# Eight of a mixer's sixteen sample states: from the second FFN's folded down products into the mixer, by ScalarE and accumulating DMAs

## The chip, the core and the metric

The kernel runs on one core of a Trainium2 chip. The metric is the device time in microseconds. The core's engines, as the profile names them: PE (TensorE, matrix products; PEld is its weight load), DVE (VectorE), ACT (ScalarE), POOL (GpSimd) and SP (SyncE, which issues most DMAs). Each engine works through its own instructions in their order and waits for others by semaphores.

## What is computed

One step of a hybrid decoder block in fp32, on 512 new tokens of a prompt and 8 sample tokens (520 columns in all), D = 1024:

```python
h = h + 0.5 * swiglu(rms_norm(h, ffn1_norm), w1_gate, w1_up, w1_down)      # FFN width 2816
m, new_pool, new_conv, new_ssm = mixer(rms_norm(h, mix_norm), states...)   # pooling heads and SSD heads
h = h + m
h = h + 0.5 * swiglu(rms_norm(h, ffn2_norm), w2_gate, w2_up, w2_down)
return rms_norm(h, final_norm), new_pool, new_conv, new_ssm
```

For each of the 8 sample tokens the SSD mixer has a state of 16 heads x 64 x 128 numbers, which one step renews: `new = exp(dt * A) * state + (dt * x) (outer product) B`. The new state is an output of its own: nothing in the step reads it, since the sample's `y` is computed from the old state and a dot product. The kernel keeps the state of sample `b` as 8 blocks of [128 partitions, 128]; blocks 0 to 3 are group g = 0 and blocks 4 to 7 are g = 1. A "state" below is one pair (b, g): 4 blocks, 256 KB. There are sixteen.

## The kernel before

Columns are handled in two halves of 260. Every fp32 product is made of three fp32r products: a weight is split into a rounded high part (ScalarE cast) and a low part (the difference), and `mm3` (L145 to L150) issues high x high, high x low and low x high. Weights come as raw 512 KB tiles, loaded by SP into a small ring of buffers (`raw_pair`, L101).

The order of the program is: FFN 1, mixer, FFN 2, final norm. A scheduler places the instructions on each engine; some are pinned by `keep_in_program_order`, and the plan strings fix the order in which the stages are written down.

**The FFNs** (`Ffn`, `stream` L534). A gate/up tile `f` (0 to 21) is computed with a two-by-two block scheme of seven products: sums of the raw weight blocks (L412 to L415), split like the weights (`shi`, `slo`), and one separate quarter of the weights (`qs`, `quarter` L432). The low part of that quarter is made either by VectorE (L237) or, for the tiles listed in `LOW_BY_DMA` (L39), by ScalarE writing the negated high part and an accumulating DMA on POOL's queue that adds the raw weights (`part_by_dma`, L230 to L233). Low parts of a tile's first weights are made by accumulating DMAs, too (L382). After tile 7 and after tile 15 the down products of the eight gate tiles before are done in the same scheme: four "folded down" tiles `Down(c, d)`, c = 0 or 1, d = 0 to 3. The last down products (`down_by_half`, L612) are plain.

**The mixer.** Its weights go through `inproj` (L879): cast, low part, 48 matmuls. `conv` (L965) makes x tiles 0 to 7 and B, C: VectorE multiplies and adds (L977), ScalarE's silu writes `X` (L979, L980). `ssd_a` (L1152) prepares one chunk and group (c, g): PE transposes B and X (`px`, L1163, 4 transposes), SP loads `ab` (L1165, three buffers), POOL subtracts (`we`, L1169), ScalarE makes the exponentials (`E` L1175, L1180, L1185, L1186), VectorE multiplies (L1193), POOL makes `xw` (L1191). `ssd_b` (L1196) has the products (`yo`, `pst`, `yd`), and POOL and VectorE update the running state `hst` (L1214, L1215). Chunks of g = 1 read x tiles 4 to 7. `sample(b, g)` (L1088) makes the sample's `y`: SP loads C's row (`cb`) and the old state (`h0`), VectorE multiplies (L1094), ScalarE sums along the row (L1097, with its output thrown away into `junk`). All this is written in the order of two strings, `CONV_PLAN` (L41) and `GATE_PLAN` (L44): `z` is a gate projection, `p`, `c`, `m` pooling, `A` and `B` the SSD parts, `s` samples, `G` and `H` the gate, `o` and `g` output projections.

**The sixteen new states** (`new_states`, L1109) are made in FFN 2. A call of the generator takes one state further: POOL's queue loads B's row, spread over partitions (`br`, L1119), and the old state (`room`, L1120); ScalarE makes `x * dt * B` for the four blocks (`so`, L1139); VectorE does `state * decay + so` (L1141); POOL's queue stores it (`out_nss`, L1143). `STATES` (L38) says where calls stand: one ahead of each of the folded down tiles (both c), one at each of the tiles 6, 17, 19, 20 and 21, and four in the last down products. The first call only loads.

Of the kernel before, what the change touches and what calls it, by code (L numbers as in the profile page):

```python
# [10 lines left out]
F32 = mybir.dt.float32  # L11
F32R = mybir.dt.float32r
AF = mybir.ActivationFunctionType
ALU = mybir.AluOpType
# [3 lines left out]
P = 128  # L18
D = 1024
SEQ = 512  # L20
NS = 8
NT = SEQ + NS
# [12 lines left out]
CHUNKS = (8, 8, 6)  # L35
LOW_ON_DVE = ((2, 0), (3, 0), (KF - 1, 1))
ON_ACT = 4
STATES = ((1, 1, 1, 1), (6, 17, 19, 20, 21), 4)  # L38
LOW_BY_DMA = {1: (2, 3, 4, 5, 6), 2: (*range(7), 9, 11)}  # L39

CONV_PLAN = (  # L41
    "b0 b1 d0 b2 b3 x0 x1 v0 d1 x2 x3 d2 X0 p0 y0 c0 A0 k0 p1 x4 m0 x5 B0 c1 p2 m1 A1 x6 c2 A2 B1 x7 X1 m2 A3"
)
GATE_PLAN = (  # L44
    "z0 B2 A4 z1 B3 p3 z2 B4 s2 z3 c3 A5 s2 z4 m3 B5 s2 A6 z5 e0 s2 G0 z6 A7 z7 B6 s2 o0 H0 s2 o1 B7 s2 o2 s2 G1 "
    "o3 g0 g1 H1 g2 g3"
)
LAST_PLAN = "h0 h2 h1 n0 h3 n1 n2 n3"
SAMPLE_U = 3 + SEQ
# [14 lines left out]
def tile_trunk_step(ctx: ExitStack, tc: tile.TileContext, ins: dict, outs: dict):  # L64
    nc = tc.nc
# [5 lines left out]
    act = ctx.enter_context(tc.tile_pool(name="act", bufs=1, side="left"))  # L71
# [184 lines left out]
    class Ffn:  # L256
# [277 lines left out]
        def stream(self, before, last_chunk):  # L534
            tiles = []
            for f in range(self.direct, KF):
                tiles.append(f)
                if f and f <= self.folded and f % CHUNKS[0] == 0:
                    tiles.extend(Down(f // CHUNKS[0] - 1, d) for d in range(KD // 2))
            prev = None  # L540
            for t in tiles:
                for _ in range(STATES[0][t.d] if not isinstance(t, int) else t in STATES[1]):
                    next(self.states, None)
                self.product(t, 1)
                if prev is not None:
                    self.product(prev, 4)
                for k, p in enumerate((2, 5, 6, 3, 7) if t in (2, KF - 1) else (5, 6, 3, 7, 2)):
                    if k == 1 and prev is not None:
                        self.close(prev)
                    self.product(t, p)  # L550
                self.gates(t)
                if t == 5 and self.later:
                    with queued(*ends[1:]):
                        self.later.pop()()
                prev = t
            self.product(KF - 1, 4)
            with tc.high_priority():
                self.close(KF - 1)
            wd = before()
            if wd is None:  # L560
                self.down(len(CHUNKS) - 1, self.folded, KF, last_chunk)
            else:
                self.down_by_half(len(CHUNKS) - 1, self.folded, last_chunk, wd)
# [48 lines left out]
        def down_by_half(self, c, lo, after, wd):  # L612
            n = KF - lo
            banks, units = {}, []
            for d in range(KD):
                if d < STATES[2]:
                    next(self.states)
# [46 lines left out]
    wx1, g1 = pool("wx1", "right"), pool("g1", "right")  # L664
# [116 lines left out]
    g2 = f2["ffn"].gp = pool("g2", "left")  # L781
# [16 lines left out]
    todo, late = [], []  # L798
# [49 lines left out]
def mixer(tc, ins, outs, e):  # L848
    nc = tc.nc
    cst, act, wp, tmp, dr, pool = (e[x] for x in ("cst", "act", "wp", "tmp", "dr", "pool"))  # L850
# [4 lines left out]
    xh, xl, _, r = nx2[0]  # L855
    xa = e["xa"][0]
    mp = pool("mx", "right")
# [191 lines left out]
    sdec = cst.tile([P, NX, NS], F32, tag="sdec", name="sdec")  # L1049
    sxdt = cst.tile([P, NX, NS], F32, tag="sxdt", name="sxdt")  # L1050
    ysm = mp.tile([P, NX, NS], F32, tag="ysm", name="ysm")
    sbc = mp.tile([P, 2, NS], F32, tag="sbc", name="sbc")
    junk = act.tile([P, NT], F32, tag="acc", name="junk")[:, :P]
    scr_bc = dr.tile([NS, 512], F32, name="scr_bc")

    def rows_bc(b, a, g):
        return scr_bc.rearrange("b (a g n) -> b a g n", a=2, g=2)[b, a, g].unsqueeze(0).to_broadcast([P, P])
# [30 lines left out]
    def sample(b, g):  # L1088
        cb = tmp.tile([P, HB], F32, tag="ta", name=f"cb{b}{g}")[:, :P]
        nc.sync.dma_start(out=cb, in_=rows_bc(b, 1, g))  # L1090
        h0 = mp.tile([P, 4, P], F32, tag="h0", bufs=4, name=f"h0_{b}{g}")
        nc.sync.dma_start(out=h0, in_=ins["state_ssm"][:, b, 4 * g : 4 * g + 4])
        tc.keep_in_program_order(
            nc.vector.tensor_tensor(out=h0, in0=h0, in1=cb.unsqueeze(1).to_broadcast([P, 4, P]), op=ALU.mult))  # L1094
        for q in range(4):
            tc.keep_in_program_order(
                nc.scalar.activation(out=junk, in_=h0[:, q], func=AF.Copy,  # L1097
                                     accum_out=ysm[:, 4 * g + q, b : b + 1]))

    def sample_y(g):  # L1100
# [8 lines left out]
    def new_states(room):  # L1109
# [10 lines left out]
            tc.keep_in_program_order(nc.gpsimd.dma_start(out=hs, in_=ins["state_ssm"][:, b, 4 * g : 4 * g + 4]))  # L1120
            return br, hs

        todo = [(b, g) for g in range(2) for b in range(NS)]
        ahead = []
        for i, (b, g) in enumerate(todo):
            if not ahead:
# [4 lines left out]
            br, hs = ahead.pop(0)  # L1131
            if "hg" in f2:
                o = f2["hg"].tile([P, 4, P], F32, tag="so", bufs=2, name=f"so{b}{g}")
            else:
                o = bank(f"so{b}{g}").rearrange("p (q n) -> p q n", q=4)
            for q in range(4):
                j = 4 * g + q
# [5 lines left out]
            tc.keep_in_program_order(nc.gpsimd.dma_start(out=outs["nss"][:, b, 4 * g : 4 * g + 4], in_=hs))  # L1143
        yield

    e["f2"]["states"] = new_states


# [137 lines left out]
    def outs_a():  # L1286
        nc.sync.dma_start(out=outs["ncp"], in_=ncp)
        nc.sync.dma_start(out=outs["ncs"], in_=sconv)
        nc.sync.dma_start(out=outs["npp"], in_=npp)
        nc.sync.dma_start(out=outs["nps"], in_=spool)  # L1290
# [20 lines left out]
        "h": lambda j: wout(cats[1], 2, j, fin),  # L1311
        "n": fill,
        "e": lambda j: outs_a(),
    }

    def run(plan):
# [98 lines left out]
```

## Time and profile before

| | |
|---|---|
| median of 3 runs | 964.78 us (963.81 to 965.73) |
| the profiled execution | 965.28 us |
| its span, first to last instruction | 963.5 us |
| granted TensorE clock, mean | 0.997 |
| busy PE / DVE / ACT / POOL | 949.7 / 850.3 / 640.7 / 142.9 us |

The span runs through FFN 1 (to about 340 us), the mixer with its output projections (about 340 to 610) and FFN 2 (to the end). The folded down tiles of FFN 1 with c = 0 lie within 80 to 160 us, those of FFN 2 with c = 0 within 680 to 760, and those with c = 1 within 820 to 880. In the view by windows each row holds the stretch, its length, then busy us and number of instructions of PE, PEld, DVE, ACT and POOL, the granted clock, the mean busy share of the DMA engines and GB/s. A timeline row holds start, duration, engine, line, operation, `out<-in`, shapes and, in brackets, idle time of the engine ahead of it and what ended that. A chain row holds start, duration, and what the time went to. A row of the DMA list ends with the size of one DMA and the median us from issue to landing.

### The profile page before, as it was taken

What the parts mean: (1) busy time and instruction counts of PE and PEld (TensorE: products, weight loads), DVE (VectorE), ACT (ScalarE), POOL (GpSimd) and SP (SyncE); (2) the same over time, 40 slices, a digit from 0 to 9 for tenths busy, and PEclk for the clock granted to TensorE, in tenths of its full rate; (3) what the DMA queues carried; (4) which work ended last, traced back from release to release, by engine and by line L of the source; (5) the groups of instructions that cost most, each with busy time, mean ns of one, the idle gap of its engine ahead of it and who ended that gap; (6) DMA issues with size and microseconds to landing.
All of it is one profiled execution on the core that took longest, in us unless ns stands there. A gap on an engine that the chain in (4) does not pass through costs nothing.

```text
span 963.5 us, 19707 instructions
## 1 busy us (share of the span) xinstructions
PE 949.7 (99%) x7676; PEld 930.3 (97%) x7676; DVE 850.3 (88%) x1456; ACT 640.7 (66%) x1208; POOL 142.9 (15%) x228
## 2 busy tenths in 40 slices
PE   9999999999999999999999999999999999999995
PEld 8999999999999999999999999999999999999995
DVE  6899899998997788789978897999889999999886
ACT  7777656676566455485676565677676676766763
POOL 0111101001010001055241000112112101122120
PEclk9999999999999999999999999999999999999998
DMA  7665654545534243362353333447656655666642
GB/s 210 182 167 145 152 156 111 138 136 143 163 112 129 73 142 110 94 199 92 117 159 121 115 117 114 117 121 166 170 154 178 154 146 147 166 192 174 187 141 90
DMA packets 53631, 137.30 MB, mean 142 GB/s; under 512 B 7641, under 2 KB 15769, under 8 KB 53537
## 3 DMA queue, kind: packets, MB, share of 16 engines
q1 hardware_dynamic: 39840, 104.18, 33.4%
q0 software_dynamic: 13424, 31.73, 17.2%
q8 instruction: 60, 0.98, 0.4%
q14 instruction: 35, 0.28, 0.1%
q10 hardware_dynamic: 272, 0.13, 0.0%
HBM read 128.67 MB, written 7.34 MB: 141 GB/s over the span
## 4 chain that ended last, share of the span: by engine, by line
PE 29%; DVE 11%; issue 4%; ACT 3%; DMA 3%; POOL 0%; DVEq 0%; ACTq 0%; POOLq 0%
PE A L150 3%; PE A L146 3%; PE A L149 3%; PE BE L149 3%; PE BE L146 2%; PE BE L150 2%; DMA raw<-in_w2d 2%; PE wo L146 2%; PE wo L150 2%; PE wo L149 2%; PE dh L150 1%; PE dh L146 1%; PE dh L149 1%; ACT junk L1097 1%; PE P L295 1%
## 5 line engine op out<-in xcount | busy, mean ns | idle before, releaser
L476 ACT COPY ac<-A 128x260 f32<-128x260 f32 x85 | 31.7, 373 | 34.8 <-PE A L150 33.6
L412 DVE TENSOR_TENSOR s<-raw 128x1024 f32<-128x1024 f32 x39 | 47.5, 1219 | 2.9 <-DMA raw<-in_w1gu 1.3
L476 ACT COPY ac<-BE 128x260 f32<-128x260 f32 x41 | 15.4, 376 | 30.0 <-PE BE L150 29.0
L146 PE MATMUL inx<-xh_mx,whi_inx 128*128 128x260 f32 x112 | 31.8, 284 | 0.0
L149 PE MATMUL inx<-xl_mx,whi_inx 128*128 128x260 f32 x112 | 31.6, 282 | 0.0
L150 PE MATMUL inx<-xh_mx,wlo_inx 128*128 128x260 f32 x112 | 31.6, 282 | 0.0
L977 DVE SCALAR_TENSOR_TENSOR A<-U,h,A 128x544 f32<-128x544 f32 x36 | 28.9, 802 | 1.3 <-ACT A L975 0.9
L295 PE MATMUL P<-x,raw 128*128 128x260 f32 x128 | 28.6, 384 | 0.0
L295 PEld LDWEIGHTS P<-x,raw 128*128 128x128 f32 x128 | 24.2, 191 | 4.0 <-DMA raw<-in_w1gu 0.4
L146 PE MATMUL wo<-catg,whi_wo 128*128 128x260 f32 x96 | 27.7, 289 | 0.0
L150 PE MATMUL wo<-catg,wlo_wo 128*128 128x260 f32 x96 | 27.2, 284 | 0.0
L149 PE MATMUL wo<-catg,whi_wo 128*128 128x260 f32 x96 | 27.1, 282 | 0.0
L1097 ACT ACTIVATE junk<-h 128x128 f32<-128x128 f32 x64 | 19.8, 309 | 10.5 <-DVE h L1094 9.0
L1139 ACT ACTIVATE so<-br,sxdt 128x128 f32<-128x128 f32 x64 | 22.5, 375 | 4.6 <-DVE room L1141 4.6
L150 PE MATMUL A<-xth_f,qs 128*128 128x260 f32 x84 | 23.8, 283 | 0.7 <-DMA qs<-in_w2gu 0.7
L146 PE MATMUL A<-xth_f,qs 128*128 128x260 f32 x84 | 23.8, 284 | 0.0
L1240 DVE TENSOR_TENSOR h<-wo,h 128x260 f32<-128x260 f32 x48 | 19.0, 416 | 5.4 <-PE wo L150 5.4
L149 PE MATMUL A<-xtl_f,qs 128*128 128x260 f32 x84 | 23.7, 282 | 0.0
L237 DVE TENSOR_TENSOR gs<-gq,gs 128x780 fp32r<-128x780 f32 (+1 forms) x28 | 23.2, 827 | 0.4 <-ACT gs L236 0.4
L146 PE MATMUL inz<-xh_mx,whi_inz 128*128 128x260 f32 x80 | 22.9, 287 | 0.0
L149 PE MATMUL inz<-xl_mx,whi_inz 128*128 128x260 f32 x80 | 22.7, 283 | 0.0
L150 PE MATMUL inz<-xh_mx,wlo_inz 128*128 128x260 f32 x80 | 22.6, 283 | 0.0
(2529 smaller groups left out, 4745.6 us busy)
## 6 DMA issues: line engine op xcount, KB each, us to landing
raw<-in_w2gu SPq DMA_DIRECT2D x44, 512.0 KB, 4.1
raw<-in_w1gu SPq DMA_DIRECT2D x41, 512.0 KB, 4.2
raw<-in_w_in SPq DMA_DIRECT2D x24, 512.0 KB, 3.6
raw<-in_w1d SPq DMA_DIRECT2D x16, 512.0 KB, 4.5
raw<-in_w2d SPq DMA_DIRECT2D x16, 512.0 KB, 4.8
raw<-in_w_out SPq DMA_DIRECT2D x12, 512.0 KB, 3.7
ab<-scr_acs SPq DMA_DIRECT2D x8, 512.0 KB, 5.0
h<-in_state_ssm SPq DMA_DIRECT2D x16, 256.0 KB, 3.3
```

The lines of the kernel that those rows point to most:

```text
L146: first = nc.tensor.matmul(ps, whi, xhi, start=start, stop=False, **kw)
L149: nc.tensor.matmul(ps, whi, xlo, start=False, stop=False, **kw)
L150: nc.tensor.matmul(ps, wlo, xhi, start=False, stop=stop, **kw)
L237: low = nc.vector.tensor_tensor(out=lo, in0=s, in1=hi.bitcast(F32), op=ALU.subtract)
L295: mm = nc.tensor.matmul(self.banks[f, u][b][:, :HB], ws(self.raw[f][:, u], j + 4 * q), xg[:, slot[q]], start=j == q == 0, stop=j == 3 and ...
L412: nc.vector.tensor_tensor(out=s1, in0=diag, in1=up0, op=ALU.add)
L476: self.copied = nc.scalar.copy(keep, out[:, :HB]).ins
L977: nc.vector.scalar_tensor_tensor(out=A[:, :n], in0=U[:, j : j + n], scalar=w(j), in1=A[:, :n], op0=ALU.mult, op1=ALU.add)
L1097: nc.scalar.activation(out=junk, in_=h0[:, q], func=AF.Copy, accum_out=ysm[:, 4 * g + q, b : b + 1]))
L1139: nc.scalar.activation(out=o[:, q], in_=br, func=AF.Copy, scale=sxdt[:, j, b : b + 1]))
L1240: nc.vector.tensor_tensor(out=h[:, d, hs], in0=ps[:, :HB], in1=h[:, d, hs], op=ALU.add)
```

## The change

- Eight states, (b, 0) for b = 0 to 7, are made by a new generator `first_states`, advanced by 17 new `t0` entries in `GATE_PLAN`. Per state: SP loads B's row (`mb`) and the old state (`mh`), one buffer each; ScalarE makes the four products `mo` and scales the four blocks of `mh` by the decay, eight instructions of 128 x 128; POOL's queue issues a DMA that adds `mo` onto `mh`; SP stores `mh`, ahead of the load of the next state.
- `mo` takes the buffer `acc` that `junk` had; the sums of `sample` write over their input instead.
- `new_states` makes the other eight. No state is left in the folded down tiles; the generator's calls stand at the tiles 16, 17, 19, 20, 21 and four in the last down products.
- `LOW_BY_DMA` loses tile 9 of FFN 2: VectorE makes that low part.
- In the order that the scheduler makes of it, PE's instructions are the same but for a few places (one `px` transpose of the first g = 1 chunk stands 22 matmuls later, one pooling product follows the transposes behind it, and near the end the products of tile 21 and of the last down tiles are interleaved differently); ScalarE has two more table loads in the mixer; on SP the states' loads and stores stand between the loads of raw weights and of `ab`; the casts, exponentials and silus of ScalarE stand around the new groups of four.

```diff
-STATES = ((1, 1, 1, 1), (6, 17, 19, 20, 21), 4)
-LOW_BY_DMA = {1: (2, 3, 4, 5, 6), 2: (*range(7), 9, 11)}
+FIRST = 8
+STATES = ((0, 0), (16, 17, 19, 20, 21), 4)
+LOW_BY_DMA = {1: (2, 3, 4, 5, 6), 2: (*range(7), 11)}
 GATE_PLAN = (
-    "z0 B2 A4 z1 B3 p3 z2 B4 s2 z3 c3 A5 s2 z4 m3 B5 s2 A6 z5 e0 s2 G0 z6 A7 z7 B6 s2 o0 H0 s2 o1 B7 s2 o2 s2 G1 "
-    "o3 g0 g1 H1 g2 g3"
+    "t0 z0 t0 B2 A4 z1 t0 B3 p3 t0 z2 t0 B4 s2 z3 t0 c3 A5 s2 z4 t0 m3 B5 s2 t0 A6 z5 t0 e0 s2 G0 z6 t0 A7 z7 B6 t0 s2 o0 t0 H0 "
+    "s2 o1 t0 B7 s2 o2 s2 t0 G1 o3 t0 g0 t0 g1 H1 g2 t0 g3"
 )
...
-                for _ in range(STATES[0][t.d] if not isinstance(t, int) else t in STATES[1]):
+                for _ in range(STATES[0][t.c] if not isinstance(t, int) else t in STATES[1]):
                     next(self.states, None)
...
-    junk = act.tile([P, NT], F32, tag="acc", name="junk")[:, :P]
...
-                nc.scalar.activation(out=junk, in_=h0[:, q], func=AF.Copy,
+                nc.scalar.activation(out=h0[:, q], in_=h0[:, q], func=AF.Copy,
                                      accum_out=ysm[:, 4 * g + q, b : b + 1]))
...
-        todo = [(b, g) for g in range(2) for b in range(NS)]
+        todo = [(b, g) for g in range(2) for b in range(NS)][FIRST:]
...
+    def first_states():
+        for b in range(FIRST):
+            br = mp.tile([P, P], F32, tag="mb", name=f"mb{b}")
+            hs = mp.tile([P, 4, P], F32, tag="mh", name=f"mh{b}")
+            nc.sync.dma_start(out=br, in_=rows_bc(b, 0, 0))
+            nc.sync.dma_start(out=hs, in_=ins["state_ssm"][:, b, :4])
+            yield
+            o = act.tile([P, NT], F32, tag="acc", name=f"mo{b}")[:, : 4 * P].rearrange("p (q n) -> p q n", q=4)
+            for q in range(4):
+                nc.scalar.activation(out=o[:, q], in_=br, func=AF.Copy, scale=sxdt[:, q, b : b + 1])
+                nc.scalar.activation(out=hs[:, q], in_=hs[:, q], func=AF.Copy, scale=sdec[:, q, b : b + 1])
+            nc.gpsimd.dma_start(out=hs, in_=o, accum_op=ALU.add)
+            yield
+            nc.sync.dma_start(out=outs["nss"][:, b, :4], in_=hs)
+
+    firsts = first_states()
...
+        "t": lambda j: next(firsts, None),
```

## The prediction

> **What bounds the kernel now.** The busy shares of the page come first, then the view by windows, which also counts the matmuls of each stretch.
>
> ```profile
> span 963.5 us, 19707 instructions
> PE 949.7 (99%) x7676; PEld 930.3 (97%) x7676; DVE 850.3 (88%) x1456; ACT 640.7 (66%) x1208; POOL 142.9 (15%) x228
> 80.00:160.00 80.00, 80.00 (x669) 80.00 (x668) 73.67 (x115) 52.19 (x84) 6.79 (x8) 1.00 0.54 141
> 680.00:760.00 80.00, 77.59 (x635) 76.39 (x634) 71.60 (x122) 52.26 (x95) 14.54 (x21) 1.00 0.67 173
> 760.00:800.00 40.00, 40.00 (x335) 40.00 (x335) 37.57 (x60) 29.12 (x49) 4.28 (x5) 1.00 0.49 131
> ```
>
> PE is the bound, at full clock: nothing gets faster unless PE waits less. Where PE never waits it starts one 260-column matmul every 80.00/669 = 0.1196 us (80 to 160, the first folded down products of the first FFN, which carry no states). In 680 to 760, the same products of the second FFN with four states inside, it starts 635: 34 fewer, so 34 x 0.1196 = 4.1 us are lost. From 760 to 800, without states, the rate is whole again. The timeline of PE shows the larger waits of that stretch (in brackets: idle time and what ended it), and the chain of waits shows two of the DMAs behind them:
>
> ```profile
> 694.09 0.39 PE L150 MATMUL A<-xth_f,slo_8d 128*128 128x260 f32 x1 [0.70 <-DVE slo_8d L136]
> 721.00 0.39 PE L150 MATMUL A_Down(c=0, d=2)_8948<-gs,wlo_Down(c=0, d=2)a 128*128 128x260 f32 x1 [0.32 <-DMA wlo_Down(c=0, d=2)a<-in_w2d]
> 734.91 0.39 PE L146 MATMUL BE_Down(c=0, d=3)_9083<-gs,shi_Down(c=0, d=3)c 128*128 128x260 f32 x1 [0.65 <-ACT BE_Down(c=0, d=3)_9083 L476]
> 754.80 0.39 PE L150 MATMUL A<-xth_f,qs 128*128 128x260 f32 x1 [0.66 <-DMA qs<-in_w2gu]
> 684.43 6.79 DMA raw<-in_w2d
> 746.77 7.99 DMA qs<-in_w2gu
> ```
>
> The releasers differ (VectorE, ScalarE, DMAs), and what they share is the state work: its loads stand beside the raw load of 6.79 us, its store beside the 7.99 us of tile 9's quarter.
>
> **Removed.** All four states leave these products, and tile 9's quarter becomes a VectorE subtraction, so the wait at 754.80 has no DMA left to wait for. I take 4.0 of the 4.1 us. The bounds are 2.0 (half the waits are the folded products' own, since this FFN frees its raw buffers later than the first) and 4.6 (also the 0.6 us of the next such stretch: 60/0.1196 = 502 matmuls against 497). I take the top of it because 80 to 160 and 760 to 800 show the same pipeline with no wait.
>
> ```profile
> 820.00:880.00 60.00, 59.89 (x497) 59.58 (x496) 57.20 (x100) 42.60 (x80) 12.46 (x19) 1.00 0.66 176
> 683.81 0.60 DVE qs L237
> ```
>
> The second folded stretch also loses its four states; the remaining eight run at tiles 17 to 21 and in the last products, as now, so beyond that bound I count nothing there. The added 0.60 us on VectorE for tile 9 (as the quarter of tile 7 in the second row) falls where state work is removed, and costs nothing as long as that is gone.
>
> **Added, in the mixer.** Each of eight states is a ring: SP loads the state (256 KB); ScalarE makes four products and scales four blocks; POOL issues an accumulating DMA; SP stores the result; then the next load, since the tile has one buffer. Instructions of an engine go in their order, so each step holds what is queued behind it: raw weights and `ab` loads on SP; casts, exponentials and silus on ScalarE; `we`, `xw` and `hst` on POOL. Prices:
>
> ```profile
> 461.43 1.26 ACT L1180 ACTIVATE ab<-ab,tok 128x128 f32<-128x128 f32 x4
> 462.60 1.03 ACT L134 CAST thi<-raw 128x1024 fp32r<-128x1024 f32 x1
> 458.76 1.28 ACT L979 ACT_TABLE_LOAD   x1
> 460.06 0.63 ACT L979 ACTIVATE X<-A 128x512 f32<-128x512 f32 x1
> h<-in_state_ssm SPq DMA_DIRECT2D x12, 256.0 KB, 2.8
> wlo_10a<-in_w1gu POOLq DMA_DIRECT2D x1, 256.0 KB, 3.6
> wlo_20a<-in_w2gu POOLq DMA_DIRECT2D x1, 256.0 KB, 5.6
> out_y<-hg SPq DMA_DIRECT2D x7, 260.0 KB, 2.2
> out_nps<-spool SPq DMA_DIRECT2D x1, 240.0 KB, 3.4
> 746.24 0.52 issue
> ```
>
> A group of four small ScalarE instructions takes 462.60 - 461.43 = 1.2 us, so 16 groups are 19 us, and the new order has two more table loads of 1.28. The ring: load 2.8 (issue to landing, 490 to 560), scaling 1.2, accumulation 3.6 (the first FFN's 256 KB ones, alone on POOL's queue), store 2.8 (between 2.2 at the quiet end and 3.4 in the mixer), hand-overs 0.5 (the piece of that name, "issue", that the chain shows ahead of a POOL DMA): 10.9, say 11. Its bounds are 9.8 (store 2.2, hand-overs nothing) and 13.5 (accumulation 5.6 as where POOL's queue shares the engines, store 3.4). The accumulations add SBUF to SBUF, which no row shows; I keep 3.6 because nothing else is on POOL's queue in the mixer.
>
> [...]
>
> Does PE wait? Its weights are cast long before: the cast at 462.60 feeds matmuls at 478.89. The tight place is the conversion of the last x tile:
>
> ```profile
> 419.00:431.00 12.00, 12.00 (x104) 11.07 (x103) 10.61 (x23) 11.98 (x28) 5.81 (x12) 1.00 0.38 114
> 429.93 1.03 ACT L134 CAST whi_inx<-raw 128x1024 fp32r<-128x1024 f32 x1
> 448.36 0.37 SPq L1165 DMA_DIRECT2D ab<-scr_acs  x1
> 453.16 0.21 ACT L1170 ACTIVATE we<-we 128x8 f32<-128x8 f32 x1 [3.94 <-POOL we L1169]
> 455.11 1.04 ACT L134 CAST whi_inp<-raw 128x1024 fp32r<-128x1024 f32 x1
> 453.16:464.68 11.52, 11.52 (x101) 10.59 (x101) 10.86 (x27) 10.38 (x22) 3.77 (x4) 1.00 0.21 63
> 464.68 0.63 ACT L979 ACTIVATE X<-A 128x512 f32<-128x512 f32 x1 [1.05 <-DVE A L977]
> 465.50 0.27 PE L1163 MATMUL px<-ident,X 128*128 128x128 f32 x1
> 478.89 0.28 PE L146 MATMUL inz<-xh_mx,thi 128*128 128x260 f32 x1
> ```
>
> 1. ScalarE is full before 431. One group of products and the first scaling stand ahead of the cast at 429.93, so the first scaling ends at 429.93 + 2 x 1.2 = 432.3, the third two rings later, at 432.3 + 22 = 454.3.
> 2. The third state's load was issued 1.2 + 2.8 = 4.0 earlier, at 450.3. The load of `ab` stands behind it on SP: 450.7 instead of 448.36. From there to `we` takes 453.16 - 448.36 = 4.8, so `we` runs at 455.5.
> 3. From `we` to the last silu (464.68) ScalarE is busy 10.38 now. The weight cast at 455.11 goes ahead of it (minus 0.94), two groups (2.4) and two table loads (2.56) come in: 14.4. The silu starts at 469.9, and the transpose that needs it 465.50 - 464.68 = 0.82 later, at 470.7.
> 4. In the new order this transpose stands 22 matmuls later on PE, due at 465.50 + 22 x 0.1196 = 468.1. PE waits **2.6 us**.
>
> Each us on the ring counts twice here. The floor is the work alone, with `we` still at 453.16: 453.16 + 14.4 + 0.82 - 468.1 = 0.3. At the ring's upper bound it is 2.6 + 2 x 2.5 = 7.6. After this place every due time is 2.6 later too, and ScalarE, though stretched, is not full:
>
> ```profile
> 464.68:506.00 41.32, 41.32 (x352) 38.53 (x351) 34.69 (x66) 28.70 (x75) 15.35 (x17) 1.00 0.46 145
> 506.00:560.00 54.00, 53.86 (x439) 51.32 (x438) 47.55 (x91) 36.65 (x115) 4.23 (x4) 1.00 0.39 126
> ```
>
> It idles 12.6 + 17.4 = 30 us, and the eight groups left need 9.6. So I count nothing more; without that cover (a slower ring) later waits add to the 7.6.
>
> **Sum.** The profiled execution took 965.28 us (span 963.5 and what lies around it). 965.28 - 4.0 + 2.6 = 963.9. It lies 0.5 above the median of the runs, 964.78, so I expect **963.4**, 0.14% less: within 0.2%, which is about what a measurement of this kernel can tell from no change (962.85 to 966.71).
>
> **Rivals.**
>
> *The mixer swallows it.* If the ring is 9.8 or less, the wait falls to its floor: 964.78 - 4.0 + 0.3 = 961.1. [...] Against: the shortest accumulation of that size takes 3.6 us, and the two table loads are certain.
>
> *The ring rules (slower).* Place: the same transpose. Price: twice what the ring is over 11. At an accumulation of 5.6 the wait is 2.6 + 2 x 2.0 = 6.6 and the time 964.78 - 4.0 + 6.6 = 967.4; with a store of 3.4 and more waits in the five later rings some 970. It decides from an accumulation of 4.3 us (wait 4.0, no gain), and from 5.25 it is slower by 0.2%. For: accumulations in the second FFN take 5.6; the stores share engines with 512 KB raw loads. Against: the first FFN's lone ones, 3.6.
>
> *Half the gain.* The folded products keep half their waits: 964.78 - 2.0 + 2.6 = 965.4.
>
> [...]
>
> **How the numbers follow.** Forecast (wait 1.5 to 5.5, whole gain) 0.40, of which 0.08 falls below 962.85 and 0.02 above 966.71; the mixer swallows it 0.32; the ring rules 0.22; half the gain 0.06. Faster 0.32 + 0.08 = 0.40, same 0.30 + 0.06 = 0.36, slower 0.22 + 0.02 = 0.24. The range, 960.6 to 968.8, takes in most of the first rival and the lower half of the second; about 0.15 is left out.
>
> **What would show it.** In the profile after: PE's count in the second FFN's first folded stretch at 669 in 80 us (right) or about 650 (half the gain); the wait before the last transpose of x, near 2.6 us, released by the silu; SP's load of the third state near 450 and the `ab` load right behind it; the accumulating DMAs near 3.6 us. Wrong would be: no PE wait in the mixer (first rival), waits at several places or landings over 5 us (second), or waits at the start of the second FFN, which I have not priced.

## The result and the profile after

The changed kernel takes 981.68 us (median of 5 runs, 980.62 to 982.53) against 964.78 us before: ratio 1.0175, 95% interval 1.0161 to 1.0189. It is slower by 1.75%, 18 us over the forecast and 13 us outside the range.

The first two lines of its page:

```profile
span 980.8 us, 19747 instructions
PE 957.3 (98%) x7676; PEld 936.0 (95%) x7676; DVE 845.4 (86%) x1425; ACT 649.2 (66%) x1241; POOL 130.9 (13%) x211
```

The page alone does not show where the 17.3 us of span went: PE runs the same 7676 matmuls and is busy 7.6 us longer (957.3 against 949.7). The view by windows does, cut at one instruction that both kernels have, a `BE` product of FFN 2's tile 1 (621.79 before, 641.34 after). Before:

```profile
420.00:621.79 201.79, 201.57 (x1609) 190.66 (x1608) 177.25 (x331) 134.77 (x318) 48.82 (x65) 1.00 0.39 121
621.79:963.50 341.71, 329.32 (x2710) 326.47 (x2710) 308.79 (x530) 233.58 (x431) 55.08 (x81) 0.99 0.58 156
```

After (the last two rows are the folded down stretches, shifted by 19.55 us):

```profile
420.00:641.34 221.34, 209.90 (x1617) 196.57 (x1615) 179.80 (x331) 152.10 (x385) 51.28 (x73) 0.97 0.49 140
641.34:980.80 339.46, 328.76 (x2710) 326.53 (x2710) 301.67 (x499) 225.16 (x398) 40.78 (x56) 0.99 0.53 142
...
699.55:779.55 80.00, 80.00 (x663) 79.62 (x662) 71.66 (x112) 51.39 (x83) 6.90 (x8) 1.00 0.54 142
...
839.55:899.55 60.00, 60.00 (x499) 59.90 (x499) 54.05 (x86) 37.96 (x64) 7.47 (x10) 1.00 0.55 143
```

Up to that product the changed kernel loses 221.34 - 201.79 = 19.55 us. From there FFN 2 takes 341.71 - 339.46 = 2.25 us less. Together that is the 17.3. Of the 19.55 us, 0.9 are not the mixer's: the first `inx` product, just ahead of 420, starts at 417.62 instead of 416.69, a difference that arises in FFN 1 and varies from one execution to the next (417.43 in e1_left_out below, 416.61 in e10_four_pinned). The mixer with its output projections takes 18.6 us longer.

Its loss has two parts. One is idle PE: 221.34 - 209.90 = 11.4 us against 0.2. The timeline of PE has the waits:

```profile
456.78 0.80 PE L147 MATMUL pm<-catp,wph 128*128 128x260 f32 x2 [2.23 <-ACT catp L1033]
...
460.05 0.58 PE L150 MATMUL pm<-catp,wph 128*128 128x260 f32 x1 [0.61 <-DVE catp L1034]
...
478.13 0.33 PE L1179 MATMUL px<-ident,X 128*128 128x128 f32 x1 [2.75 <-ACT X L980]
...
510.10 0.39 PE L147 MATMUL pm<-catp,wph 128*128 128x260 f32 x1 [0.91 <-ACT catp L1033]
...
514.87 1.19 PE L1221 MATMUL pst<-xw,bt 128*128 128x512 f32 x1 [2.28 <-ACT bt L1174]
...
545.70 0.58 PE L147 MATMUL wo<-catp,thi 128*128 128x260 f32 x1 [2.25 <-DVE scm L1176]
```

The prediction had one wait, the one at 478.13, and its size (2.75 us against 2.6). The others it did not have.

The second part is the granted clock. Windows of 1 us around the first of these waits and around the one at 478.13 (the third number from the end is the clock):

```profile
456.00:457.00 1.00, 0.22 (x1) 0.23 (x2) 1.00 (x2) 0.72 (x4) 0.00 (x0) 0.87 0.21 51
457.00:458.00 1.00, 1.00 (x5) 1.00 (x6) 1.00 (x2) 0.00 (x0) 0.00 (x0) 0.50 0.87 349
...
462.00:463.00 1.00, 1.00 (x6) 1.00 (x6) 1.00 (x3) 0.27 (x3) 0.83 (x2) 0.50 0.08 14
463.00:464.00 1.00, 1.00 (x9) 1.00 (x7) 1.00 (x7) 1.00 (x5) 0.45 (x2) 0.72 1.10 197
...
477.00:478.00 1.00, 0.00 (x0) 0.00 (x0) 0.40 (x1) 0.99 (x3) 0.00 (x0) 1.00 1.11 197
478.00:479.00 1.00, 0.87 (x7) 0.87 (x8) 0.78 (x3) 0.98 (x3) 0.50 (x3) 1.00 0.31 51
```

After the first wait PE works at half its clock: the rows from 456 to 464 lose 0.13 + 6 x 0.50 + 0.28 = 3.4 us. Behind the waits at 514.87 and 545.70 the same rows lose 1.7 us each; behind the one at 478.13 nothing. That is 6.8 us; about 0.5 of it falls into idle time that is counted already (the 0.61 us ahead of 460.05 above all), so 6.3 us are left, more than half as much as the idle time itself. 11.2 + 6.3 + 0.9 = 18.4 of the 19.55 us. The rest (1.1 us) is not placed. The `pst` of 514.87, 1.19 us against a median of 0.59 for its line, ran at a clock of 0.50 and is in the 1.7 us already.

**What PE waited for.** The waits of ScalarE, SP and POOL between 424 and 550, from the view of waits (total us, times, longest):

```profile
POOL mh L1157 <- ACT mh L1156: 35.0, 7, 11.4
ACT mh L1156 <- DMA mh<-in_state_ssm: 10.2, 4, 3.3
ACT mo L1155 <- DMA mh<-mo: 9.8, 3, 4.6
SPq L1159 <- DMA mh<-mo: 45.4, 7, 9.3
```

All four are steps of the ring, waiting for the step before them at the head of an engine's queue. In the median the DMAs behind them (SP's and POOL's queues, 424 to 550) are near what the prediction took; the fourth line, of the tile `mh`, shows how far they spread:

```profile
mh<-mo POOLq DMA_DIRECT2D x8, 256.0 KB, 3.4
out_nss<-mh SPq DMA_DIRECT2D x8, 256.0 KB, 2.3
mh<-in_state_ssm SPq DMA_DIRECT2D x7, 256.0 KB, 2.9
DMA to landing us min/median/max: 2.0/3.3/6.8
```

Long ones stand ahead of two of PE's long waits. Ahead of the wait at 456.78 the accumulation of 432.99 took 5.4 us and the load of 440.64 took 6.8 (and the next load, of 454.63, 5.2); ahead of the wait at 514.87 the load of 507.65 took 5.6. The load of 440.64 stands beside a raw load of 512 KB that SP had issued 0.5 us earlier and that took 6.6 us. What it would have taken without that neighbour no run shows.

How the wait at 456.78 comes about can be read across three timelines. SP:

```profile
438.48 0.34 SPq L1159 DMA_DIRECT2D out_nss<-mh  x1
439.74 0.32 SPq L1150 DMA_DIRECT2D mb<-scr_bc  x1
440.16 0.39 SPq L143 DMA_DIRECT2D raw<-in_w_in  x1
440.64 0.38 SPq L1151 DMA_DIRECT2D mh<-in_state_ssm  x1
```

SP stands at the first store until 438.48; then four transfers start within 2.2 us, and the state's load lands only near 447.5. ScalarE:

```profile
438.44 1.28 ACT L1155 ACTIVATE mo<-mb,sxdt 128x128 f32<-128x128 f32 x4 [3.57 <-DMA mh<-mo]
...
447.56 1.28 ACT L1156 ACTIVATE mh<-mh,sdec 128x128 f32<-128x128 f32 x4 [3.34 <-DMA mh<-in_state_ssm]
...
452.47 1.28 ACT L1155 ACTIVATE mo<-mb,sxdt 128x128 f32<-128x128 f32 x4 [2.53 <-issue]
...
454.50 1.28 ACT L1186 ACT_TABLE_LOAD   x1
...
456.12 0.60 ACT L1033 CAST catp<-PW 128x512 fp32r<-128x512 f32 x1
```

ScalarE stands still three times for the ring (3.57, 3.34, 2.53 us; for the third the profile names no releaser, but the accumulation out of the same buffer `mo`, issued at 449.14, landed just before, as SP's store behind it went out at 452.46), and the cast of `catp`, which PE needs at 454.6, comes at 456.12. POOL:

```profile
449.14 0.87 POOL L1157 DMA_DIRECT2D mh<-mo  x1 [3.45 <-ACT mh L1156]
449.75 1.56 POOL L1019 TENSOR_TENSOR PW<-PW 128x648 f32<-128x648 f32 x1
```

The pooling sums, from which that cast is made, stand behind the accumulating DMA. The chain of waits between 425 and 562 sums this up by line, and the ring's DMAs lead it. In the kernel before, the same view is led by the samples' sums on ScalarE (8.1%), and no DMA is among its first lines. After:

```profile
by line: DMA mh<-in_state_ssm 10.2%; DMA mh<-mo 8.1%; issue 7.8%; DMA out_nss<-mh 7.0%; ACT mh L1156 4.6%; PE wo L147 2.7%; ACT mo L1155 2.7%; ACT ab L1196 2.7%; DMA cb<-scr_bc 2.6%; PE psr_y L196 2.6%; ACT E L1191 2.5%; ACT h L1097 2.5%; P
```

### The profile page after: what moved, and what is told of

It is laid out like the page before. It is cut to its first block, busy times and chain, and to the rows that moved or that the text cites. A ratio compares the mean times of both kernels' runs of the same rounds, so it can differ in the third digit from the quotient of the medians.

```text
span 980.8 us, 19747 instructions
## 1 busy us (share of the span) xinstructions
PE 957.3 (98%) x7676; PEld 936.0 (95%) x7676; DVE 845.4 (86%) x1425; ACT 649.2 (66%) x1241; POOL 130.9 (13%) x211
## 4 chain that ended last, share of the span: by engine, by line
PE 36%; DMA 6%; DVE 5%; ACT 4%; issue 2%; SPq 0%; DVEq 0%; POOL 0%; ACTq 0%; POOLq 0%
PE A L147 3%; PE A L151 3%; PE A L150 3%; PE BE L150 3%; PE BE L151 3%; PE BE L147 2%; PE wo L147 2%; PE wo L151 2%; PE wo L150 2%; DMA raw<-in_w2gu 2%; DMA mh<-in_state_ssm 1%; PE dh L151 1%; PE dh L147 1%; PE dh L150 1%; DMA mh<-mo 1%
## 5 line engine op out<-in xcount | busy, mean ns | idle before, releaser
L137 DVE TENSOR_TENSOR tlo<-raw,thi 128x1024 fp32r<-128x1024 f32 (+1 forms) x14 | 17.4, 1243 | 10.4 <-ACT thi L135 10.4
L1097 ACT ACTIVATE h<-h 128x128 f32<-128x128 f32 x64 | 18.9, 296 | 9.8 <-DVE h L1094 9.8
```

Of the source, the lines that this page charges most:

```text
L137: low = nc.vector.tensor_tensor(out=l, in0=src, in1=h.bitcast(F32), op=ALU.subtract)
L1097: nc.scalar.activation(out=h0[:, q], in_=h0[:, q], func=AF.Copy, accum_out=ysm[:, 4 * g + q, b : b + 1]))
```

## The experiments

The theories, as they stood after the traces had been compared. **A**: ScalarE, SP and POOL stand in order behind the round trips of a ring with one buffer each. **B**: ScalarE's own added work is too much for this stretch. **C**: the added DMA bytes slow the raw and `ab` loads. Ratios are against the kernel before on the same chip, each with its 95% interval.

### Each part alone

**e1_left_out**: no first states at all.

```diff
     def first_states():
-        for b in range(FIRST):
+        return
+        yield
...
```

> The changed kernel with the eight first states left out altogether (their part of the new state is not written): what the mixer pays is gone, what the second FFN gains stays. In the profile after, the second FFN starts 19.5 us later than before and the end comes 17.3 us later, so the FFN keeps 2.2 us: all theories expect about 962.5 us (960.8 if the whole 4.0 us of the prediction is there).

963.23 us, ratio 0.998 (0.997 to 0.9991). As expected: the gain in FFN 2 is about 2 us, not 4.0. The view by windows of this kernel has the part from the same `BE` product on at 339.20 us, 2.5 less than before:

```profile
622.00:961.20 339.20, 328.17 (x2710) 326.31 (x2710) 301.84 (x499) 225.41 (x398) 40.70 (x56) 0.99 0.53 142
```

**e2_act_only**: ScalarE's work on one resident tile.

```diff
-        for b in range(FIRST):
-            br = ...; hs = ...; two loads; yield
+        br = ...; hs = ...; two loads once; yield
+        for b in range(FIRST):
             o = ...; eight activations
-            nc.gpsimd.dma_start(out=hs, in_=o, accum_op=ALU.add)
             yield
-            nc.sync.dma_start(out=outs["nss"][:, b, :4], in_=hs)
+            yield
```

> ScalarE's 64 small instructions stay at their places, but they work on one resident tile: no loads, accumulations or stores after the first load (the first states' output is not written). Theory A (ScalarE, SP and POOL stand in order behind the round trips of a ring with one buffer): ScalarE never waits for a DMA, so 962 to 966 us. Theory B (ScalarE's own 22 us of added work and table loads are too much for this stretch): 975 to 982. Theory C (the added DMA traffic slows the raw and ab loads): as without states, 962 to 964.

964.36 us, ratio 1.0001 (0.999 to 1.0011): some 1 to 2 us above e1. Theory B falls, more clearly than planned: with nothing to wait for, the scheduler packed all of it into the tightest stretch, as the view of the tile `mh` shows (first and last start):

```profile
L1156 ACT ACTIVATE mh<-mh,sdec x32: 386/396/414, 434.0 to 467.1; 128x128 f32<-128x128 f32 x32
```

**e3_dma_only**: the loads, accumulations and stores without ScalarE's work.

```diff
-            o = ...; eight activations
+            if b == 0:
+                o = ...; four activations
             nc.gpsimd.dma_start(out=hs, in_=o, accum_op=ALU.add)
```

> The opposite half: loads, accumulating DMAs and stores of all eight states stay, ScalarE's scaling and products go (one product is made once; the values written are not the states). Theory A: ScalarE is free of waits, SP and POOL still stand for the ring, now of about 9 us (load 3, accumulation 3.5, store 2.5): part of the loss, 965 to 973 us. Theory B: 962 to 964. Theory C: most of the loss, 975 to 982.

978.89 us, ratio 1.0142 (1.0111 to 1.0172). Most of the loss is there with ScalarE free, more than theory A gave, and as much as theory C did. The timelines of POOL, ScalarE and PE, from an execution of 976.30 us, show why:

```profile
454.40 0.87 POOL L1157 DMA_DIRECT2D mh<-mo  x1 [7.54 <-DMA mh<-in_state_ssm]
455.00 1.56 POOL L1019 TENSOR_TENSOR PW<-PW 128x648 f32<-128x648 f32 x1
```

```profile
456.78 0.84 ACT L976 ACTIVATE A<-U,h 128x544 f32<-128x544 f32 x1 [11.27 <-POOL U L971]
...
461.56 0.62 ACT L1033 CAST catp<-PW 128x512 fp32r<-128x512 f32 x1 [1.57 <-POOL PW L1024]
```

```profile
462.24 0.80 PE L147 MATMUL pm<-catp,wph 128*128 128x260 f32 x2 [7.25 <-ACT catp L1033]
```

POOL stands 7.54 us at the accumulation, which has no data yet; the pooling sums and the convolution's `U` stand behind it; ScalarE waits 11.27 us for `U`; PE waits 7.25 us. Three engines are late for one DMA that was issued too early.

**e7_no_sp**: ScalarE's work and the accumulations, on one resident tile.

```diff
-        for b in range(FIRST):
-            br = ...; hs = ...; two loads; yield
+        br = ...; hs = ...; two loads once; yield
+        for b in range(FIRST):
...
             nc.gpsimd.dma_start(out=hs, in_=o, accum_op=ALU.add)
             yield
-            nc.sync.dma_start(out=outs["nss"][:, b, :4], in_=hs)
+            yield
+        nc.sync.dma_start(out=outs["nss"][:, 0, :4], in_=hs)
```

> ScalarE's work and the accumulating DMAs stay, with their waits for one another, on one resident tile; the loads and stores of SP go, but for the first load and one store at the end (the first states' output is not written). If SP's queue or the traffic is what costs: 963 to 967 us. If POOL's queue and ScalarE's waits for the accumulation are: 972 to 981.

972.0 us, ratio 1.0064 (1.0044 to 1.0084): with SP out of the ring there are still some 8 us of loss over e1. The accumulations are enough for that, at the head of POOL's queue (26.7 us behind ScalarE's scaling) and in ScalarE's waits for them (5.2).

**e6_vector**: POOL out of it.

```diff
-                nc.scalar.activation(out=hs[:, q], in_=hs[:, q], func=AF.Copy, scale=sdec[:, q, b : b + 1])
-            nc.gpsimd.dma_start(out=hs, in_=o, accum_op=ALU.add)
+                nc.vector.scalar_tensor_tensor(out=hs[:, q], in0=hs[:, q], scalar=sdec[:, q, b : b + 1],
+                                               in1=o[:, q], op0=ALU.mult, op1=ALU.add)
```

> The whole new state, but VectorE does decay times state plus product in one pass per block (32 instructions) in place of ScalarE's scaling and the accumulating DMA: POOL has no part in it, and the ring is a DMA shorter. SP's loads and stores stay. If POOL's queue is what costs: 963 to 968 us. If SP's queue is: 973 to 980, less what the shorter ring gives. If the traffic is (a third less): 970 to 975.

975.26 us, ratio 1.0109 (1.0085 to 1.0132). So neither POOL nor SP is the one queue: each of e3, e6 and e7 takes one engine out, and each keeps a large part of the loss. In e6 the same work stands on VectorE instead, and one of its two long PE waits (3.35 us at 482.88) ends with VectorE; what these 32 instructions cost by themselves is not separated.

**e5_traffic** and **e16_traffic_pinned**: nearly the same bytes, with no other work waiting for them. B's row is loaded once, and a write of 256 KB to memory stands in place of each accumulation (in e5 these writes share one place and wait for one another on POOL, 8.8 us in all). In e16 each of the DMAs is pinned.

```diff
+        o = ...; four activations once
         for b in range(FIRST):
             nc.sync.dma_start(out=hs, in_=ins["state_ssm"][:, b, :4])
             yield
-            eight activations
-            nc.gpsimd.dma_start(out=hs, in_=o, accum_op=ALU.add)
+            nc.gpsimd.dma_start(out=away, in_=o)
             yield
-            nc.sync.dma_start(out=outs["nss"][:, b, :4], in_=hs)
+            nc.sync.dma_start(out=outs["nss"][:, b, :4], in_=o)
```

> The traffic alone, with nothing that waits for it: SP loads each old state into a tile that nobody reads, POOL's queue writes 256 KB from a constant tile to a scratch in memory in place of each accumulation, SP stores the same constant tile (the values written are not the states; ScalarE's work is left out but for one group). Theory C (the bytes slow the raw and ab loads): most of the loss of the run with DMAs only, 973 to 979 us. Theory A2 (what costs is the instructions that stand at the head of SP's and POOL's queues waiting for the ring): 963 to 966.

964.37 us, ratio 0.9987 (0.9976 to 0.9999). The scheduler had drawn its loads together at 357 to 378 and its stores at 428 to 433; only POOL's writes (427 to 459) lay spread over the ring's first stretch. In e16 each stands at its call:

> The traffic alone once more, now pinned at the calls of the plan, since in the first run of this kind the scheduler had drawn the loads together at 357 to 378 us and the stores at 428 to 433: per state a load that nobody reads, a write from a constant tile to a scratch in memory by POOL's queue, a store of the same tile (the values written are not the states). Theory A2: 963 to 966 us, against 986.8 of the pinned run whose steps wait for each other at the same calls. Theory C (bytes): 975 to 985.

963.1 us, ratio 0.998 (0.9968 to 0.9992), the same as with no states. The stores now stand spread, by the view of the tile `mo`:

```profile
L1160 SPq DMA_DIRECT2D out_nss<-mo x8: 338/432/652, 469.9 to 528.8; - x8
```

Theory C falls: bytes that nothing waits for cost nothing here (963.1 us, against 963.23 in e1_left_out). e16's loads took 4.1 us in the median and up to 6.3, so long transfers are free there; in the ring the same lengths are waited for. What is left of A is sharper (**A2**): what costs is an instruction at the head of a queue whose data is not there.

### Buffers, places and distances

**e4_buffers**: the whole change with the samples' four buffers for `mh` and two for `mo`.

```diff
-            hs = mp.tile([P, 4, P], F32, tag="mh", name=f"mh{b}")
+            hs = mp.tile([P, 4, P], F32, tag="h0", bufs=4, name=f"mh{b}")
             two loads
+            if len(live) > 1:
+                nc.sync.dma_start(out=outs["nss"][:, b - 2, :4], in_=live.pop(0))
             yield
-            o = act.tile([P, NT], F32, tag="acc", ...)
+            o = mp.tile(..., tag="mh") if b % 2 else act.tile(..., tag="acc")
...
-            nc.sync.dma_start(out=outs["nss"][:, b, :4], in_=hs)
```

> The whole change, but with buffers: the old states load into the four buffers of the samples' tile, the products alternate between two, the next load stands ahead of the store, and each store comes one state later. The same ScalarE work and the same DMAs. Theory A: no engine waits for the ring any more, most of the 19.5 us of the mixer goes: 964 to 970 us. Theory B: 976 to 982, as ScalarE's work is unchanged. Theory C: 976 to 982, as the traffic is unchanged.

980.98 us, ratio 1.0165 (1.015 to 1.0181). Theory A as it stood fails here: these buffers do not help. The ring's waits are shorter than in the change (424 to 550: POOL 13.1 us for ScalarE's scaling instead of 35.0, SP 13.6 for the accumulations instead of 45.4), but the longest waits of PE are as long, at other places (2.84 us at 449.70, 2.85 at 582.30). The states now share buffers with the samples, whose loads wait 12.2 us for the states' stores; how much of the loss is that sharing is not separated.

**e8_four_lagged** and **e10_four_pinned**: four states, each step one call behind the one it needs. In e10 the same instructions are also pinned.

```diff
-FIRST = 8
-STATES = ((0, 0), (16, 17, 19, 20, 21), 4)
+FIRST = 4
+STATES = ((0, 1), (16, 17, 19, 20, 21), 4)
...
                 eight activations
+            yield
             nc.gpsimd.dma_start(out=hs, in_=o, accum_op=ALU.add)
             yield
             nc.sync.dma_start(out=outs["nss"][:, b, :4], in_=hs)
+            yield
```

> Four states instead of eight in the mixer, in the same seventeen calls, with each step (load, ScalarE, accumulation, store) one call behind the one that it needs; the other four stand in the folded down products with c = 1, as before. The first folded products stay empty. Theory A2 (instructions that wait at the head of a queue): nothing waits, so 963 to 966 us. If the number of states decides (traffic or work): half the loss, 970 to 974.

972.05 us, ratio 1.0065 (1.0045 to 1.0084): a miss for A2. But the lag was not there: nothing in the generator is pinned, the scheduler drew the steps together again (stores at 438.6 to 477.5), and POOL still waited at each of the four accumulations (424 to 480):

```profile
POOL mh L1158 <- ACT mh L1156: 17.8, 4, 5.7
```

> As the run with four lagged states (972.05), with the steps pinned: now the lag of one call is really there in the queues. Theory A2: 963 to 966 us, no wait of PE in the mixer. If pinning changes nothing: 971 to 973.

963.72 us, ratio 0.9989 (0.9981 to 0.9998). The only edit against e8 is the pinning (`tc.keep_in_program_order` around each of the steps); it is worth 7 to 8 us. PE's largest wait in the mixer is 0.54 us. Three of the four accumulations are issued without a wait, and the fourth, which waits, has nothing of weight behind it (POOL's timeline):

```profile
472.14 0.90 POOL L1158 DMA_DIRECT2D mh<-mo  x1
...
499.64 0.88 POOL L1158 DMA_DIRECT2D mh<-mo  x1
...
526.57 0.87 POOL L1158 DMA_DIRECT2D mh<-mo  x1
...
565.02 0.86 POOL L1158 DMA_DIRECT2D mh<-mo  x1 [22.81 <-ACT mh L1156]
```

The chain of waits from 455 to 605 has no DMA of the ring among its first lines (the changed kernel's has them there, with 9.3, 7.4 and 6.4%):

```profile
by line: PE wo L147 14.3%; PE wo L151 13.9%; PE wo L150 13.9%; PE inz L147 8.7%; PE inz L150 8.7%; PE inz L151 8.7%; PE psr_y L196 4.8%; PE P L296 4.7%; PE yd L1226 3.4%; PE pst L1223 2.9%; PE yo L1220 2.4%; DVE A L978 1.6%; PE inp L147 1.4
```

This version beats both kernels, the one before by 0.1%. Steps of the ring still wait in it (POOL 22.8 us, SP 10.4 and 9.9, ScalarE 3.7, between 455 and 575), but nothing that PE needs soon stands behind them.

Pinning changes two things at once: the ring starts near 461 instead of 427, and its steps stand apart. Two runs take one of them away each.

**e13_four_tight**: e10 without the lag (the change's own generator, pinned, with four states).

> Four states, pinned and at the late place as in the run of 963.72, but without the lag: the accumulation is issued right behind ScalarE's group, and the next load right behind the store (9 calls instead of 16). If the lag is what frees the queues: 968 to 975 us. If the late place alone does it: 963 to 965.

967.91 us, ratio 1.0025 (1.0016 to 1.0035): 3.5 us above e10. The late place does not do it alone. The stores stand at 474.4 to 525.4, 17.0 us a turn.

**e14_four_early**: e10 with ten of its sixteen calls in the convolution plan; the other six are the first six `t0` of `GATE_PLAN`.

```diff
-    ... A0 k0 p1 x4 m0 x5 B0 c1 p2 m1 A1 x6 c2 A2 B1 x7 X1 m2 A3
+    ... A0 k0 t0 p1 t0 x4 t0 m0 x5 t0 B0 t0 c1 p2 t0 m1 A1 t0 x6 t0 c2 A2 t0 B1 x7 t0 X1 m2 A3
```

> Four states, pinned and lagged as in the run of 963.72, but at the early place: the calls stand in the convolution plan behind k0, between the x tiles, where the scheduler put the ring of the change. If the place (the last x tiles, where ScalarE, POOL and SP each have work due within a few us) is what makes the ring dear: 968 to 975 us. If the lag is enough anywhere: 963 to 966.

968.86 us, ratio 1.0036 (1.0024 to 1.0048): 4.5 us above e10. The lag of one call does not do it alone either. But this run does not change the place alone: its stores stand at 439.4 to 493.1, 17.9 us a turn, as tight as e13, where e10 has 31. What the early place costs by itself is not separated. The turns of the four-state runs go with their times: 12.9 us in e8 (7 to 8 us above e10), 17.0 and 17.9 in e13 and e14, 31 in e10.

### Eight states

**e9_pinned**: the change, pinned, nothing else.

```diff
-            nc.gpsimd.dma_start(out=hs, in_=o, accum_op=ALU.add)
+            tc.keep_in_program_order(nc.gpsimd.dma_start(out=hs, in_=o, accum_op=ALU.add))
```

(and so for each of the loads, activations and stores)

> The whole change, with one difference: the loads, ScalarE's groups, the accumulations and the stores of the eight first states are pinned where the plan writes them (as those of the samples are), so the scheduler can't move them ahead. The work, the DMAs and the buffers are those of the change; the ring starts about 30 us later and its steps stand further apart. Theory A2 (steps that the scheduler put at the heads of SP's, POOL's and ScalarE's queues before their data is there): most of the 19.5 us of the mixer goes, 964 to 970 us. If work, traffic or the single buffers decide: 976 to 982, as after.

986.75 us, ratio 1.0227 (1.021 to 1.0243): worse than the change, and the clearest miss for A2. Pinning alone is no cure; it only frees a queue where the distance is kept. **e15_eight_lagged** keeps it as far as the plan has room, pinned too, and **e17_six_lagged** does so with six states:

```diff
             eight activations
+            yield
             nc.gpsimd.dma_start(out=hs, in_=o, accum_op=ALU.add)
             yield
             nc.sync.dma_start(out=outs["nss"][:, b, :4], in_=hs)
```

with 27 and 19 entries `t0` spread over `GATE_PLAN` (e15 uses 25 of them); e17 has `FIRST = 6` and `STATES = ((0, 1), (17, 20, 21), 4)`.

> All eight states of the change, pinned, in 25 calls that are spread from the first gate projection to the last output projection; the accumulation stands one call behind ScalarE's group, the store one behind that, and only the next load stands right behind the store. Theory A2: the number of states costs nothing as long as no step waits at the head of its queue, 962 to 966 us. If eight are too many for the late place: 970 to 985, as the pinned run without lag (986.75).

983.89 us, ratio 1.0189 (1.017 to 1.0208).

> Six states, pinned, lagged and late, in 19 calls, between the four that cost nothing (963.7) and the eight that cost 19 us (983.9). If each turn of the single-buffer ring needs about as much time as four states have (26 us each) before its steps stop waiting: 970 to 978. If the cost sets in only with the eighth: 963 to 966.

973.24 us, ratio 1.0077 (1.0059 to 1.0096). The view of the tile `mh` gives the stores' first and last start, in e15:

```profile
L1160 SPq DMA_DIRECT2D out_nss<-mh x8: 338/343/384, 475.6 to 585.9; - x8
```

and in e10:

```profile
L1160 SPq DMA_DIRECT2D out_nss<-mh x4: 338/400/525, 475.5 to 568.4; - x4
```

A turn of the ring is (585.9 - 475.6)/7 = 15.8 us with eight states and (568.4 - 475.5)/3 = 31 us with four; with six it is 20.4 (474.6 to 576.4). At 31 us no step that PE depends on soon waits. At 15.8 the steps wait for each other again however they are ordered: POOL 34.9 us for ScalarE's scaling, and ScalarE 5.9 us for the loads and 8.4 for B's rows (the longest wait of PE is then 6.37 us, at 583.80). The stretch from 461 to 590 carries four turns of this single-buffer ring for nothing, and not six.

### The two small edits

**e12_tile9**: the kernel before, tile 9's quarter on VectorE.

```diff
-LOW_BY_DMA = {1: (2, 3, 4, 5, 6), 2: (*range(7), 9, 11)}
+LOW_BY_DMA = {1: (2, 3, 4, 5, 6), 2: (*range(7), 11)}
```

> The kernel before with tile 9's quarter on VectorE as its only edit. The prediction's claim is that it takes the 0.7 us wait for that quarter's DMA away (964.1 us) and costs nothing; if VectorE's 0.60 us is on the path there, 964.8 to 965.5.

965.48 us, ratio 1.0004 (0.9992 to 1.0015): it costs nothing that can be told, and by itself gains nothing.

**e11_in_tiles**: no state in the mixer, the four of the first folded products at gate tiles.

```diff
-STATES = ((1, 1, 1, 1), (6, 17, 19, 20, 21), 4)
+STATES = ((0, 1), (6, 9, 11, 13, 15, 17, 19, 20, 21), 4)
```

> No state in the mixer: all sixteen stay in the second FFN as before, but the four of the first folded down products go to the gate tiles 9, 11, 13 and 15, one each; tile 9's quarter on VectorE. If only the folded products are too tight for a state: 962 to 963.5 us, about as with the first states left out (963.2). If a state costs about 0.5 to 1 us wherever it stands in this FFN: 964 to 966.

971.19 us, ratio 1.0072 (1.0059 to 1.0086), above both expectations. In the profiled execution, the fastest of six (968.34 us), the first folded stretch is free (661 matmuls from 680 to 760), and the next two pay for it:

```profile
760.00:826.00 66.00, 64.54 (x530) 63.65 (x529) 62.94 (x105) 49.76 (x91) 10.76 (x16) 1.00 0.62 156
826.00:880.00 54.00, 52.67 (x433) 52.07 (x432) 49.70 (x91) 36.72 (x69) 12.31 (x19) 1.00 0.70 179
```

At the full rate these would be 552 and 451 matmuls; 40 x 0.1196 = 4.8 us are lost. Of these two places the folded products are the better one for a state.

## Why the prediction was wrong

**The bound and the rate** were right: PE bounds, and where it does not wait it starts a matmul every 0.1196 us.

**"Removed: 4.0 of the 4.1 us"**: right in kind, too large. The first folded stretch went from 635 to 663 matmuls in 80 us (3.3 us), the second from 497 to 499 (0.2). But new waits stand outside them: 0.78 us at 690.69, for an earlier tile's quarter that comes by DMA, 0.25 at 906.84 and 0.23 at 909.98. 2.25 us are left in the trace after, and e1 has about 2 us in its times. The lower bound, 2.0, was the better value; the forecast took the top without asking where a freed engine waits next. Tile 9's part (nothing) was right: e12.

**"10.9, say 11"** (the ring): in the median each DMA was priced well (2.9 + 3.4 + 2.3 us against 2.8 + 3.6 + 2.8), and the accumulations are near the row that the prediction leaned on (3.6; the eight of them took 3.3 to 5.9). Yet the stores are issued at 438.48 to 532.72, (532.72 - 438.48)/7 = 13.5 us a turn. Turns add up means, not medians: over these seven, loads took 4.1, accumulations 3.8 and stores 2.7 us, 10.5 together against 9.2 (read one by one from the view of DMAs). That leaves 13.5 - 10.5 - 1.2 = 1.8 us of hand-overs, taken as 0.5 from one piece of the chain (746.24), just ahead of which the same chain has pieces of that name of 4.31 and 2.43 us (738.49, 742.91). So both were too small, by about 1.3 us each. The turn is the prediction's own upper bound, for which its sum gives a wait of 7.6 and 964.78 - 4.0 + 7.6 = 968.4 us: the size of the ring does not explain 981.68.

**"The tight place is the conversion of the last x tile"**: right about this place, where PE waited 2.75 us, released by that silu. But the steps towards it all came late: the third load at 454.63 (450.3 predicted), `ab` at 455.14 (450.7), `we` at 462.87 (455.5), the silu at 477.45 (469.9). The transpose was due at 475.38 instead of 468.1, since PE itself had lost some 7 us by then, and the steps were late by about as much. That the wait has the predicted size is luck.

**"So I count nothing more"** is the step that failed. The prediction said that each step of the ring "holds what is queued behind it", and then followed this at one place, along ScalarE's busy time. It counted ScalarE's idle 30 us as cover. What the runs showed in its place: the cost is not in busy time (e2, ScalarE's work alone, 1 to 2 us) and not in bytes that nothing waits for (e16, nothing), but in the time that ScalarE, POOL and SP stand with a step of the ring at the head of their queues (10.2 + 9.8 = 20.0, 35.0 and 45.4 us in the trace after), as far as due work stands behind it. The first such place, the wait at 456.78 for the pooling cast, lies ahead of the one that the prediction followed. Idle time in the middle of such a stretch is no cover, as the in-order queue spends it waiting. An engine on which a ring step waits passes it on to whoever needs what stands behind: e3 shows one DMA's 7.54 us go through POOL and ScalarE to a PE wait of 7.25.

**"The ring rules (slower)"** was the rival that happened, at 22%, but with the wrong switch and price. It was to decide from an accumulation of 4.3 us; the median is 3.4 and the ring rules nevertheless. Both of its signs came, waits at several places and landings over 5 us (accumulations of 5.4 and 5.9, loads of 6.8, 5.2 and 5.6). Its 967 to 970 us counted only the one wait and "more waits in the five later rings" as about 3 us; by the timeline they are 0.91 + 2.28 + 2.25 = 5.4 us of idle PE in the three long ones behind 478.13, 2.23 + 0.61 = 2.8 ahead of it, and the clock on top.

**The clock** was in no step: 6.3 us of the loss. The first wait's 2.23 us, with the 0.61 behind it, cost 3.1 us more.

**The table switches**: as the rows of before said, each takes 1.28 us and the next instruction starts at once (in the trace after, the load of 454.50 ends at 455.78 and the next instruction starts at 455.80).

What stays open: how much a second set of buffers would be worth at the late place (e4 had them at the early one, shared with the samples), what the early place costs at e10's turn, how much of the ring's length is due to the raw loads beside its DMAs, and where the last 1.1 us of the mixer's loss lies.

## What to carry to other kernels

In these runs a DMA round trip that is cut into steps on several in-order queues cost nothing only where each step reached the head of its queue with its data there, or with nothing behind it that was due before the data came (e10_four_pinned, 963.72 us; the same four states without the lag, e13_four_tight, 967.91). So list, for each step, the instructions behind it and when they are due, on every engine it touches, and not just the busy time that it adds. The distance between the steps has to be written into the order (here pinning and a lag, 7 to 8 us for four states), since a scheduler may draw them together (e8_four_lagged, stores at 438.6 to 477.5); and it needs room: here a turn of 31 us was free, and turns of 17 to 20 us were not. Price a turn by the mean of its transfers at that place, not by the median (here 10.5 us against 9.2).

## What the runs showed of the hardware

In the changed kernel PE's waits of 2.23, 2.28 and 2.25 us (456.78, 514.87 and 545.70) go with half the granted clock: in windows of 0.1 us it is 0.50 from 456.8 to 463.5, from 514.8 to 518.1 and from 545.5 to 548.8. The wait of 2.75 us at 478.13 does not: the clock is 1.00 in each window of 1 us from 474 to 483. So the length of a wait does not decide it by itself; what does was not shown.

Idle PE in two other runs shows no loss of clock: in e2_act_only PE idles 3.0 us of the 205.8 from 420 to 625.82 (205.82 - 202.81), in e10_four_pinned 0.6 of the 202.3 from 420 to 622.3 (202.30 - 201.69), and the mean granted clock of both stretches is 1.00.
